# Spreading the first expert-table blocks over the second loop, pinning its last blocks, and laying the gate matrix out by tile of eight experts

## The chip, the cores and the metric

The kernel runs on one core of one Trainium2 chip. The metric is the device time of one execution in microseconds; the time before is the median of 3 runs.

## What is computed

A decoder block over 512 tokens of 1024 channels, all float32: a Conformer convolution and a sliding-window attention run beside each other, are merged by gates and added to the residual; then comes PEER, a mixer that picks experts by product keys. Cut to what matters here:

```python
h  = rmsnorm(x, norm1_g);  z = h @ w_in + b_in          # split into value, gate, q, k, v, two merge gates
x  = x + merged(conv, attention) @ w_out
h2 = rmsnorm(x, norm2_g)
q  = (h2 @ w_peer_q)                                     # 8 heads x 2 halves x 128
sc = einsum(q, sub_keys);  top 16 of each half; best 16 of their 256 sums -> expert_idx, gate (softmax)
a  = gelu(einsum("ced,cd->ce", u_emb[expert_idx], h2))   # 128 chosen of 16384 experts per token
x  = x + einsum("ce,ced->cd", gate * a, v_emb[expert_idx])
out = rmsnorm(x, final_g)
```

## The kernel before, in words

Tokens come in four blocks of 128. Every product is made in float32r from split operands: x = hi + lo, and a product is hi*hi + lo*hi + hi*lo. `load_w` fetches a 512 KB block of weights on SP's queue (`wraw`, 3 buffers), makes `whi` on ACT (L131) and `wlo` either on DVE (L137) or by an accumulating DMA from GpSimd (L134, L135, while `by_dma` is set); both have 4 buffers.

The first stage normalises the four token blocks, transposes them into `hT` and multiplies by `w_in` (42 blocks). The first two weight blocks go through `halves` (L159), which runs both over the first 256 tokens and then both over the second 256, so that TensorE begins before all of `hT` is there.

PEER treats the token blocks in two ways. Block 0 (`ROW_CHUNKS`) gathers its expert rows by indirect DMA (`by_rows`, L644): 128 slots over the `pu` table, each a multiply and sum on DVE (L651), a gelu, then 128 slots over the `pv` table, added up on DVE (L659) in `acc`, which starts as the residual `x2d`. Blocks 1 to 3 are dense: they multiply by all 16384 experts in 128 blocks of 128.

- U block i (`u_pieces`, L671): 24 matmuls of 384 columns over `put[i]`, gelu into `ga[i]`. 43 buffers of `ga` let U run ahead of V.
- The gate matrix: for each dense block, `build_g` (L599) builds 128 x 128 pictures of the softmax gates, four tokens a step, and stores 16 tokens at a time (`gst`, 2 buffers) to DRAM as `gb` (L632), 8 stores per block, 24 in all. `load_gates` (L679) brings back the part of eight experts (`gl`, 2 buffers), three loads per tile, one per dense block.
- V block i (`v_operands`, L687; `v_products`, L698): w = gate part times `ga[i]` on DVE (L690), split on ACT and DVE (L694, L695), then 18 matmuls of 512 columns over `pv[i]` (L701 to L703) that add into six PSUM banks `vacc` over all 128 blocks.

Order of work: eight heads (`head(h)`: scores on PE, L525; top 16 on DVE, L509 and on), each followed by `U_HEADS[h]` U blocks, 25 in all; then `keys` (L584) and `build_g` for three blocks, with 17 more U blocks threaded between the steps matmul by matmul and pinned in program order, so that 42 (`AHEAD`) are done; then 128 rounds. A round does one U block as long as there are any (rounds 0 to 85), one V block, and some slots of `by_rows`: 2.51 a round while there are U blocks, 1.03 after. The last two V blocks are taken together (L765) after the rows are finished and the residual of the three dense blocks has been loaded (L764). Then `vacc` is added (L774) and `finish` (L663) normalises and stores. The tile framework orders the instructions of each engine by a simulation of its own; program order and the dependencies are its input, and only pinned instructions keep their written order. Each engine and each DMA queue runs its instructions in order.

Of the kernel before, what the change touches and what calls it, by code (L numbers as in the profile page):

```python
# [9 lines left out]
F32 = mybir.dt.float32  # L10
# [3 lines left out]
AF = mybir.ActivationFunctionType  # L14
OP = mybir.AluOpType
AX = mybir.AxisListType

P = 128
D = 1024
KB = D // P  # L20
S = 512
# [12 lines left out]
ROW_CHUNKS = (0,)  # L34
# [4 lines left out]
CAND = 80  # L39

AHEAD = 42
U_HEADS = (4, 3, 3, 3, 3, 3, 3, 3)
U_PIECE = 3.6
ROWS = 4
GT = 16
GI = 8
R_G = 0.0
ROWS_U, ROWS_V = 1.48, 1.03
UC = 3
N_TAPS = 7  # L50
XT = 8
# [11 lines left out]
J_VAL, J_GATE, J_Q, J_K, J_V, J_GC, J_GA = 0, 8, 16, 24, 25, 26, 34  # L63
# [16 lines left out]
def body(ctx: ExitStack, tc: tile.TileContext, a, out):  # L80
    nc = tc.nc
# [4 lines left out]
    dram = ctx.enter_context(tc.tile_pool(name="dram", bufs=1, space=bass.MemoryType.DRAM))  # L86
# [7 lines left out]
    x2d = [dram.tile([P, D], F32, name=f"x2d{b}") for b in range(NB)]  # L94
    h2d = {b: dram.tile([P, D], F32, name=f"h2d{b}") for b in ROW_CHUNKS}
    NG = P // GT
    gv = {}
    for b in BUILT:
        gv[b] = dram.tile([P, NG, P, GT], F32, name=f"gb{b}")

    ident = const.tile([P, P], F32, name="ident")
    pc = const.tile([P, C_N], F32, name="pc")
# [9 lines left out]
    pace = [None]  # L112
# [43 lines left out]
        products(p, w, x)  # L156
        return p

    def halves(srcs, x):  # L159
        w = [load_w(t) for t in srcs]  # L160
        ps2 = [psum("mm") for _ in srcs]
        for c in (slice(0, S // 2), slice(S // 2, S)):
            for p, v in zip(ps2, w):
                products(p[:, c], v, [t[:, :, c] for t in x])
        return ps2
# [30 lines left out]
    def chunk(b):  # L196
        return slice(b * P, (b + 1) * P)
# [10 lines left out]
    warm = small.tile([P, 1], F32, name="warm", bufs=1)  # L208
# [16 lines left out]
    hT = pair_x("hT")  # L225
# [76 lines left out]
    def glu(j):  # L302
        if j >= UC:
            conv(KB * TAPS, j - UC)
        if j == 0:
            ps0 = halves([a["w_in"][J_GATE], a["w_in"][J_VAL]], hT)
            by_dma[0] = True
        pg = ps0[0] if j == 0 else zblock(J_GATE + j)
        sg = fr.tile([P, S], F32, name="sg")
        nc.scalar.activation(sg, pg, AF.Sigmoid, bias=bias(J_GATE + j))  # L310
        pv = ps0[1] if j == 0 else zblock(J_VAL + j)
        uc = fr.tile([P, HALO + S], F32, name="uc", bufs=UC)
        nc.vector.memset(uc[:, :HALO], 0.0)
        nc.vector.scalar_tensor_tensor(uc[:, HALO:], pv, bias(J_VAL + j), sg, op0=OP.add, op1=OP.mult)
        ucs[j] = uc
# [110 lines left out]
    p = psum("ot")  # L426
# [4 lines left out]
    for j in range(KB):  # L431
# [4 lines left out]
        else:  # L436
            nc.scalar.activation(sq, y[:, j], AF.Square)
            nc.vector.tensor_tensor(ysum, ysum, sq, op=OP.add)
    p = psum("ot")
    nc.tensor.matmul(p, ones, ysum, start=True, stop=True)  # L440
    r = rstd_of(p, D, [fr.tile([P, S], F32, name="ln_v", tag="qs", bufs=2),
                       fr.tile([P, S], F32, name="ln_t", tag="sg"),
                       fr.tile([P, S], F32, name="ln_r", tag="qs", bufs=2)])
# [7 lines left out]
    for j in range(KB):  # L451
        p = mm_block(a["w_ao"][j], oT)
        nc.vector.tensor_tensor(sga[:, j], sga[:, j], p, op=OP.mult)
    mT = pair_y("m")
    for j in range(KB):
        p = mm_block(a["w_co"][j], yT)
# [142 lines left out]
    def build_g(b):  # L599
        n = BUILT.index(b)  # L600
        p = psum("tr")
        nc.tensor.transpose(p[:, :P], gate[:, b], ident)
        gT = rt.tile([P, P], F32, name="gT", bufs=2)
        nc.scalar.activation(gT, p[:, :P], AF.Copy)
        high = P // LOW
        for g in range(P // GT):
            if g * GT % XS == 0:
                xa = gp.tile([P, XS, high], F32, name="xa")
                xb = gp.tile([P, XS, LOW], F32, name="xb")
                cs = slice(g * GT, g * GT + XS)  # L610
                for t, w, k in ((xa, high, 0), (xb, LOW, 1)):
                    nc.vector.tensor_tensor(t, keyT[:, k, n, cs, None].to_broadcast([P, XS, w]),
                                            iota[:, None, :w].to_broadcast([P, XS, w]), op=OP.is_equal)
                nc.vector.tensor_tensor(xa, xa, gT[:, cs, None].to_broadcast([P, XS, high]), op=OP.mult)
            st = gp.tile([P, P, GT], F32, name="gst", bufs=2)
            for t0 in range(0, GT, XT):
                c = slice(g * GT + t0, g * GT + t0 + XT)
                cx = slice(c.start % XS, c.start % XS + XT)
                yt = gp.tile([P, XT, P], F32, name="yt", tag="yt", bufs=XB)
                nc.vector.tensor_tensor(yt, keyT[:, 2, n, c, None].to_broadcast([P, XT, P]),  # L620
                                        iota[:, None, :].to_broadcast([P, XT, P]), op=OP.is_equal)
                xt = gp.tile([P, XT, high, LOW], F32, name="xt", tag="xt", bufs=XB)
                nc.vector.tensor_tensor(xt, xa[:, cx, :, None].to_broadcast([P, XT, high, LOW]),
                                        xb[:, cx, None, :].to_broadcast([P, XT, high, LOW]), op=OP.mult)
                for t1 in range(0, XT, 4):
                    p = psum(("sc", "ot")[t1 // 4 % 2]).rearrange("p (t i) -> p t i", t=4)
                    for t in range(4):
                        nc.tensor.matmul(p[:, t], yt[:, t1 + t], xt[:, t1 + t].rearrange("p a b -> p (a b)"),
                                         start=True, stop=True)
                    nc.scalar.activation(st[:, :, t0 + t1:t0 + t1 + 4].rearrange("p i t -> p t i"), p, AF.Copy)  # L630
                    yield
            nc.sync.dma_start(gv[b][:, g], st)  # L632

    def gathered(table, b, s):
        r = rows.tile([P, D], F32, name="row", bufs=ROWS)
# [8 lines left out]
    def by_rows():  # L644
        for b in ROW_CHUNKS:
            h = rows.tile([P, D], F32, name="hrow", tag="acc")
            nc.sync.dma_start(h, h2d[b])
            dots = small.tile([P, SLOTS], F32, name="dots", bufs=1)
            for s in range(SLOTS):
                r = gathered(a["pu"], b, s)  # L650
                nc.vector.scalar_tensor_tensor(r, r, 1.0, h, op0=OP.mult, op1=OP.mult, accum_out=dots[:, s:s + 1])  # L651
                yield
            nc.scalar.activation(dots, dots, AF.Gelu)
            nc.vector.tensor_tensor(gate[:, b], dots, gate[:, b], op=OP.mult)
            acc = rows.tile([P, D], F32, name="acc", tag="acc")
            nc.sync.dma_start(acc, x2d[b])
            for s in range(SLOTS):
                r = gathered(a["pv"], b, s)
                nc.vector.scalar_tensor_tensor(acc, r, gate[:, b, s:s + 1], acc, op0=OP.mult, op1=OP.add)  # L659
                yield  # L660
            finish(b, acc)

    def finish(b, acc):  # L663
        o = wp.tile([P, D], F32, name="wraw", bufs=WRAW)
        rmsnorm(o, acc, gf)
        nc.sync.dma_start(out[chunk(b), :], o)
# [12 lines left out]
    def load_gates(i, blocks=range(ND)):  # L679
        if i < P:  # L680
            if 0 in blocks:
                gl[i // GI] = vp.tile([P, NU // GT, GI, GT], F32, name="gl", bufs=2)
            for n in blocks:
                b = DENSE[n]
                nc.sync.dma_start(gl[i // GI][:, n * NG:(n + 1) * NG], gv[b][:, :, i:i + GI, :])

    def v_operands(i):  # L687
        v = load_w(a["pv"][chunk(i), :])
# [6 lines left out]
        nc.vector.tensor_tensor(wl3, w, wh3.bitcast(F32), op=OP.subtract)  # L695
        return v, (wh, wl)

    def v_products(i, n, v, w):  # L698
        for q in range(2):
            p, ns = vacc[2 * n + q], slice(q * 512, (q + 1) * 512)  # L700
            nc.tensor.matmul(p, w[0][:, chunk(n)], v[0][:, ns], start=(i == 0), stop=False)  # L701
            nc.tensor.matmul(p, w[0][:, chunk(n)], v[1][:, ns], start=False, stop=False)  # L702
            pace[0] = nc.tensor.matmul(p, w[1][:, chunk(n)], v[0][:, ns], start=False, stop=(i == P - 1))  # L703

    def v_steps(*steps):
        ops = [(i, v_operands(i)) for i in steps]
        for n in range(ND):
            for i, (v, w) in ops:
                v_products(i, n, v, w)

    ups = iter(range(P))

    def up(n):
        for _ in range(n):
            i = next(ups, None)
            if i is not None:
                for _ in u_pieces(i, load_w(a["put"][i])):
                    pass
# [31 lines left out]
    due = 0.0  # L750
    load_gates(0)
    last = {}
    for i in range(P):
        up(1)
        if 0 <= i % GI - GL_AT < ND:
            load_gates(i - i % GI + GI, (i % GI - GL_AT,))
        if i < P - 2:
            v_steps(i)
        elif i == P - 2:
            for _ in rowgen:  # L760
                pass
            for n, b in enumerate(DENSE):
                last[n] = rows.tile([P, D], F32, name="row", bufs=ROWS)
                nc.sync.dma_start(last[n], x2d[b])  # L764
            v_steps(i, i + 1)  # L765
        due += ((ROWS_U if i + AHEAD < P else 0.0) + ROWS_V) * len(ROW_CHUNKS)
        while due >= 1:
            due -= 1
            next(rowgen, None)
# [59 lines left out]
```

## Time and profile before

| | |
|---|---|
| median of 3 runs | 1771.82 us (1771.04 to 1774.27) |
| the profiled execution | 1772.01 us, span 1770.2 us |
| PE (TensorE matmul) busy | 1707.9 us, 96% of the span |
| DVE (VectorE) busy | 1355.1 us, 77% |
| ACT (ScalarE) busy | 898.5 us, 51% |
| GpSimd busy | 461.3 us, 26% |
| DMA | 444.86 MB, mean 251 GB/s |

The span runs from the first to the last instruction of the profiled execution; its time has another 1.8 us around it. The share of busy time is a mean over stages with different limits. PEld is PE's weight load, which overlaps PE. The clock in a row is the share of full speed that was granted to TensorE, whose two levels are 1.2 and 2.4 GHz.

### The profile page before, as it was taken

To read this page: it belongs to the slowest core of one execution; us is meant where nothing else is said; L and a number is where in the kernel's file an instruction comes from. 1 tells how busy PE (TensorE), PEld (TensorE's weight loads), DVE (VectorE), ACT (ScalarE), POOL (GpSimd) and SP (SyncE) were. 2 spreads that over 40 slices of the span, in tenths; PEclk is the share of its full clock that TensorE was granted. 3 is DMA by queue.
4 is the path that set the end of the run, shared out by engine and by line. 5 is a ranking of instruction groups with operands and counts; after the bars stand their busy time and mean duration, and the time that the engine had idled before them with its cause. 6 is when DMAs were issued, how large, how long until landed. Compare 5 with 4: busy or idle time off the path is not lost. (4 is left out here: it accounts for less than half of the span.)

```text
span 1770.2 us, 24879 instructions
## 1 busy us (share of the span) xinstructions
PE 1707.9 (96%) x8892; PEld 1504.4 (85%) x8892; DVE 1355.1 (77%) x2659; ACT 898.5 (51%) x1287; POOL 461.3 (26%) x374
## 2 busy tenths in 40 slices
PE   7999999999999996999899999999999999999996
PEld 6887777788899996999799999999999999977875
DVE  6999994545589998887677777777868778777775
ACT  6448999654656565887333333333333333333332
POOL 1111010110111110000334434433434534344330
PEclk9999998999999998999999999999999999999998
DMA  8996553885999994988889989888879889788873
GB/s 240 231 223 148 134 125 71 191 229 174 248 229 211 215 211 121 282 277 286 293 283 335 320 290 315 320 289 320 316 271 333 302 307 331 284 300 296 299 275 128
DMA packets 165708, 444.86 MB, mean 251 GB/s; under 512 B 14544, under 2 KB 66256, under 8 KB 162512
## 3 DMA queue, kind: packets, MB, share of 16 engines
q0 software_dynamic: 53280, 194.01, 41.2%
q1 hardware_dynamic: 112304, 249.26, 39.3%
q8 instruction: 70, 1.15, 0.3%
q14 instruction: 54, 0.44, 0.1%
HBM read 410.44 MB, written 29.88 MB: 249 GB/s over the span
## 5 line engine op out<-in xcount | busy, mean ns | idle before, releaser
L131 ACT ACTIVATE whi<-wraw 128x1024 fp32r<-128x1024 f32 x346 | 365.3, 1057 | 378.0 <-PE mm L146 188.7
L146 PE MATMUL mm<-tTh,whi 128*128 128x384 f32 (+2 forms) x1168 | 398.4, 342 | 1.5 <-ACT wlo L134 1.4
L146 PE MATMUL mm<-tTl,whi 128*128 128x384 f32 (+2 forms) x1168 | 398.6, 342 | 0.2 <-DVE tTl L194 0.2
L137 DVE TENSOR_TENSOR wlo<-wraw,whi 128x1024 fp32r<-128x1024 f32 x232 | 282.7, 1222 | 68.4 <-ACT whi L131 54.5
L636 POOL DMA_INDIRECT row<-pv,eidx x128 | 185.6, 1450 | 268.4 <-DVE acc L659 257.7
L636 POOL DMA_INDIRECT row<-pu,eidx x128 | 176.5, 1379 | 271.3 <-DVE row L651 243.3
L146 PE MATMUL mm<-tTh,wlo 128*128 128x384 f32 (+2 forms) x1168 | 240.5, 341 | 0.1
L694 ACT ACTIVATE wh<-gl 128x384 fp32r<-128x384 f32 x128 | 67.1, 525 | 329.8 <-PE ot L702 289.0
L146 PEld LDWEIGHTS mm<-tTh,whi 128*128 128x128 f32 x1168 | 220.0, 188 | 10.0 <-ACT wlo L134 1.8
L146 PEld LDWEIGHTS mm<-tTl,whi 128*128 128x128 f32 x1168 | 219.8, 188 | 8.3 <-DVE tTl L194 0.4
L146 PEld LDWEIGHTS mm<-tTh,wlo 128*128 128x128 f32 x1168 | 202.9, 188 | 4.2 <-DMA wlo<-w_pq 0.3
L659 DVE SCALAR_TENSOR_TENSOR acc<-row,gate,acc 128x1024 f32<-128x1024 f32 x128 | 164.0, 1282 | 12.3 <-DMA row<-pv,eidx 7.7
L296 DVE SCALAR_TENSOR_TENSOR yconv<-uc,pc,yconv 128x512 f32<-128x512 f32 x240 | 169.0, 746 | 0.4
L651 DVE SCALAR_TENSOR_TENSOR row<-row,hrow 128x1024 f32<-128x1024 f32 x128 | 154.4, 1220 | 8.6 <-DMA row<-pu,eidx 8.0
L146 PE MATMUL mm<-hTh,whi 128*128 128x512 f32 (+1 forms) x352 | 136.7, 391 | 1.1 <-ACT hTh L193 0.8
L146 PE MATMUL mm<-hTl,whi 128*128 128x512 f32 (+1 forms) x352 | 136.1, 389 | 1.4 <-DVE hTl L194 1.4
L690 DVE TENSOR_TENSOR gl<-gl,ga 128x384 f32<-128x384 f32 x128 | 62.0, 553 | 88.6 <-DMA gl<-gb 88.6
L134 ACT ACTIVATE wlo<-whi 128x1024 fp32r<-128x1024 f32 x114 | 120.2, 1055 | 9.7 <-PE mm L146 9.0
L695 DVE TENSOR_TENSOR wl<-gl,wh 128x384 fp32r<-128x384 f32 x128 | 71.0, 555 | 67.9 <-ACT wh L694 63.2
L701 PE MATMUL tr<-whi,wh 128*128 128x512 f32 x256 | 101.2, 397 | 9.1 <-ACT wh L694 5.3
L135 POOL DMA_DIRECT2D wlo<-w_in x40 | 34.9, 872 | 268.6 <-ACT wlo L134 212.3
L703 PE MATMUL tr<-whi,wl 128*128 128x512 f32 x256 | 96.4, 402 | 8.3 <-DVE wl L695 8.3
(255 smaller groups left out, 3174.1 us busy)
## 6 DMA issues: line engine op xcount, KB each, us to landing
wraw<-put SPq DMA_DIRECT2D x128, 512.0 KB
wraw<-pv SPq DMA_DIRECT2D x128, 512.0 KB
gb<-gst SPq DMA_DIRECT2D x24, 1024.0 KB
gl<-gb SPq DMA_DIRECT2D x48, 512.0 KB
wraw<-w_in SPq DMA_DIRECT2D x42, 512.0 KB
wlo<-put POOLq DMA_DIRECT2D x42, 512.0 KB
wlo<-w_in POOLq DMA_DIRECT2D x40, 512.0 KB
wraw<-w_out SPq DMA_DIRECT2D x16, 512.0 KB
```

The source lines that it names most:

```text
L131: nc.scalar.activation(hi, raw, AF.Copy)
L134: nc.scalar.activation(lo, hi.bitcast(F32), AF.Copy, scale=-1.0)
L137: nc.vector.tensor_tensor(lo, raw, hi.bitcast(F32), op=OP.subtract)
L146: pace[0] = nc.tensor.matmul(p, v[:, k * P:(k + 1) * P], t, start=(n == 0), stop=(n == len(terms) - 1))
L296: nc.vector.scalar_tensor_tensor(y[:, j], uc[:, t:t + S], w, y[:, j], op0=OP.mult, op1=OP.add)
L636: ins = nc.gpsimd.indirect_dma_start(out=r, out_offset=None, in_=table, in_offset=bass.IndirectOffsetOnAxis(ap=eidx[:, ROW_CHUNKS.index(b) ...
L651: nc.vector.scalar_tensor_tensor(r, r, 1.0, h, op0=OP.mult, op1=OP.mult, accum_out=dots[:, s:s + 1])
L659: nc.vector.scalar_tensor_tensor(acc, r, gate[:, b, s:s + 1], acc, op0=OP.mult, op1=OP.add)
L694: nc.scalar.activation(wh3, w, AF.Copy)
L695: nc.vector.tensor_tensor(wl3, w, wh3.bitcast(F32), op=OP.subtract)
L701: nc.tensor.matmul(p, w[0][:, chunk(n)], v[0][:, ns], start=(i == 0), stop=False)
L703: pace[0] = nc.tensor.matmul(p, w[1][:, chunk(n)], v[0][:, ns], start=False, stop=(i == P - 1))
```

## The change

The U blocks that are not yet done when V begins (86) are spread over 126 rounds at 86.5/126 a round, in place of one a round in the first 86. Row slots go at one rate, 2.07 a round. The heads get 3, 3, 3, 3, 3, 2, 3, 5 U blocks. `halves` can take other cuts, and the first use takes three: 128, 128 and 256 tokens. `gb` lies in DRAM by tile of eight experts, so that a load of `gl` reads 4 KB in one piece for each of 128 partitions, and a store writes 16 pieces of 512 bytes for each. In `by_rows` the first V slot writes `acc` with a multiply, and the residual is loaded and added at the end. In `v_products` the last two V blocks are ordered by bank (n, then q, then block), and pinned. After the last U block, ACT runs a Square and a Sqrt on one column.

```diff
-U_HEADS = (4, 3, 3, 3, 3, 3, 3, 3)
+U_HEADS = (3, 3, 3, 3, 3, 2, 3, 5)
-ROWS_U, ROWS_V = 1.48, 1.03
+ROWS_V = 2.07
...
-        gv[b] = dram.tile([P, NG, P, GT], F32, name=f"gb{b}")
+        gv[b] = dram.tile([P, P // GI, NG, GI, GT], F32, name=f"gb{b}")
...
-    def halves(srcs, x):
+    def halves(srcs, x, cuts=(slice(0, S // 2), slice(S // 2, S))):
...
-        for c in (slice(0, S // 2), slice(S // 2, S)):
+        for c in cuts:
...
-            ps0 = halves([a["w_in"][J_GATE], a["w_in"][J_VAL]], hT)
+            ps0 = halves([a["w_in"][J_GATE], a["w_in"][J_VAL]], hT,
+                         (chunk(0), chunk(1), slice(S // 2, S)))
...
-            nc.sync.dma_start(gv[b][:, g], st)
+            nc.sync.dma_start(gv[b][:, :, g], st.rearrange("p (a i) t -> p a i t", i=GI))
...
-            nc.sync.dma_start(acc, x2d[b])
             for s in range(SLOTS):
                 r = gathered(a["pv"], b, s)
-                nc.vector.scalar_tensor_tensor(acc, r, gate[:, b, s:s + 1], acc, op0=OP.mult, op1=OP.add)
+                if s == 0:
+                    nc.vector.tensor_scalar(acc, r, gate[:, b, s:s + 1], None, op0=OP.mult)
+                else:
+                    nc.vector.scalar_tensor_tensor(acc, r, gate[:, b, s:s + 1], acc, op0=OP.mult, op1=OP.add)
                 yield
+            r = rows.tile([P, D], F32, name="row", bufs=ROWS)
+            nc.sync.dma_start(r, x2d[b])
+            yield
+            nc.vector.tensor_tensor(acc, acc, r, op=OP.add)
             finish(b, acc)
...
-                nc.sync.dma_start(gl[i // GI][:, n * NG:(n + 1) * NG], gv[b][:, :, i:i + GI, :])
+                nc.sync.dma_start(gl[i // GI][:, n * NG:(n + 1) * NG], gv[b][:, i // GI])
...
+    def v_products(i, n, q, v, w, pin):
+        p, ns = vacc[2 * n + q], slice(q * 512, (q + 1) * 512)
+        for t, (wk, vk) in enumerate(((0, 0), (0, 1), (1, 0))):
+            pace[0] = nc.tensor.matmul(p, w[wk][:, chunk(n)], v[vk][:, ns], start=(i == 0 and t == 0),
+                                       stop=(i == P - 1 and t == 2))
+            if pin:
+                tc.keep_in_program_order(pace[0])
+
+    def v_steps(*steps, pin=False):
         ops = [(i, v_operands(i)) for i in steps]
         for n in range(ND):
-            for i, (v, w) in ops:
-                v_products(i, n, v, w)
+            for q in range(2):
+                for i, (v, w) in ops:
+                    v_products(i, n, q, v, w, pin)
...
+    ahead, share, tabled = AHEAD, 0.0, []
     for i in range(P):
-        up(1)
+        share += (P - AHEAD + 0.5) / (P - 2)
+        while share >= 1 or ahead <= min(i + 1, P - 1):
+            share -= 1
+            ahead += 1
+            up(1)
...
-        elif i == P - 2:
+        if ahead >= P and not tabled:
+            tabled.append(i)
+            nc.scalar.activation(warm, ga[P - 1][:, 0:1], AF.Square)
+            nc.scalar.activation(warm, warm, AF.Sqrt)
+        if i == P - 2:
...
-            v_steps(i, i + 1)
-        due += ((ROWS_U if i + AHEAD < P else 0.0) + ROWS_V) * len(ROW_CHUNKS)
+            v_steps(i, i + 1, pin=True)
+        due += ROWS_V * len(ROW_CHUNKS)
```

## Rows read from the trace of the kernel before

**Rows 1.** Waits of PE, whole span: us in total, times, longest.

```profile
PE tr L596 <- DVE k_p L592: 13.2, 2, 10.2
PE tr L703 <- DVE wl L695: 8.3, 4, 3.0
...
PE tr L701 <- ACT wh L694: 5.3, 1, 5.3
PE tr L701 <- ACT whi L131: 3.9, 1, 3.9
```

**Rows 2.** Windows: length, busy us of PE, PEld, DVE, ACT, POOL; clock, DMA, GB/s.

```profile
857.00:862.00 5.00, 5.00 (x12) 3.98 (x13) 5.00 (x10) 1.63 (x3) 0.00 (x0) 0.50 0.89 291
1564.00:1744.00 180.00, 171.69 (x738) 140.21 (x736) 133.03 (x154) 59.10 (x80) 58.90 (x41) 0.98 0.79 276
1747.00:1753.00 6.00, 5.13 (x12) 4.03 (x13) 4.26 (x8) 1.76 (x2) 0.00 (x0) 0.51 0.22 90
```

**Rows 3.** Waits of DVE from 1564 to 1744 us.

```profile
DVE gl L690 <- DMA gl<-gb: 25.1, 4, 7.5
```

**Rows 4.** Timeline of DVE at the first V block: start, us, instruction, [idle before].

```profile
855.72 3.84 DVE L690 TENSOR_TENSOR gl<-gl,ga 128x384 f32<-128x384 f32 x8 [8.62 <-DMA gl<-gb]
```

**Rows 5.** DMA queues, 1572.5 to 1575 us: packets, MB, share of 16 engines.

```profile
q1 hardware_dynamic: 1482, 0.75, 100.0%
```

**Rows 6.** DMA queues, 836.5 to 838.5 us, while a store of `gb` runs.

```profile
q1 hardware_dynamic: 109, 0.88, 103.8%
```

**Rows 7.** DMA queues, 848 to 851 us, gathers beside loads of `gl`.

```profile
q0 software_dynamic: 313, 1.15, 93.7%
q1 hardware_dynamic: 218, 0.11, 12.0%
```

**Rows 8.** Timeline of SP's queue behind the first loads of `gl`.

```profile
843.35 7.64 SPq L647 DMA_DIRECT2D hrow<-h2d  x1
```

**Rows 9.** Waits of DVE in the heads, 466 to 690 us.

```profile
DVE sv L509 <- PE sc L525: 21.9, 15, 6.2
```

**Rows 10.** Timeline of DVE before the scores of head 1 and of head 4.

```profile
504.64 0.30 DVE L509 MAX8 sv<-sc 128x8 f32<-128x128 f32 x1 [5.45 <-PE sc L525]
...
580.32 0.30 DVE L509 MAX8 sv<-sc 128x8 f32<-128x128 f32 x1 [1.40 <-PE sc L525]
```

**Rows 11.** Timeline of PE at the start, and the first plain f32 products.

```profile
12.65 1.97 PE L192 MATMUL tr<-ident,h 128*128 128x128 f32 x8 [2.49 <-DVE hTl L194]
...
22.67 1.03 PE L192 MATMUL tr<-ident,h 128*128 128x128 f32 x8
...
27.95 0.39 PE L146 MATMUL mm<-hTl,whi 128*128 128x256 f32 x1 [0.22 <-DVE hTl L194]
...
686.92 2.08 PE L628 MATMUL sc<-xt,yt 128*128 128x128 f32 x8 [0.44 <-DVE xt L623]
```

**Rows 12.** Window of the building of the gate matrix (columns as in rows 2).

```profile
690.00:840.00 150.00, 150.00 (x1133) 150.00 (x1133) 125.25 (x127) 123.12 (x141) 11.26 (x13) 1.00 0.83 264
```

**Rows 13.** The tile `gst`: its stores, and idle time of its engines until.

```profile
L632 SPq DMA_DIRECT2D gb<-gst x24: 319/320/327, 695.7 to 835.5; - x24
...
  DMA gb<-gst: 18.0, 14
```

**Rows 14.** Timeline of SP's queue at the end.

```profile
1731.44 6.86 SPq L764 DMA_DIRECT2D row<-x2d  x3
```

**Rows 15.** Timeline of ACT at the end.

```profile
1745.37 1.28 ACT L172 ACT_TABLE_LOAD   x1
...
1760.35 1.04 ACT L182 ACTIVATE wraw<-row 128x1024 f32<-128x1024 f32 x1
```

**Rows 16.** The chain that ended last: start, us, what.

```profile
1758.01 0.24 PE ot L703
```

**Rows 17.** Timeline of DVE at the end.

```profile
1758.86 1.28 DVE L774 TENSOR_TENSOR row<-row,ot 128x512 f32<-128x512 f32 x2
...
1765.10 1.29 DVE L184 SCALAR_TENSOR_TENSOR wraw<-row,n_r,g 128x1024 f32<-128x1024 f32 x1
```

More of the change, by code (lines that the diff above doesn't have):

```diff
@@ L696, in v_operands @@
         return v, (wh, wl)
[L698 to L705, printed above, removed]
+    def v_products(i, n, q, v, w, pin):
[6 more added lines that the diff above has]
+    def v_steps(*steps, pin=False):
         ops = [(i, v_operands(i)) for i in steps]
         for n in range(ND):
-            for i, (v, w) in ops:
-                v_products(i, n, v, w)
+            for q in range(2):
+                for i, (v, w) in ops:
+                    v_products(i, n, q, v, w, pin)
     ups = iter(range(P))
```

## The prediction

> **What bounds the kernel now.** I read the list of waits of PE first, because PE is the engine that works in every stage: what it waits for can be won, the rest is its own work. The long waits that the change touches are four [rows 1]: 13.2 us in two pieces (10.2 the longer) before the transposes of `keys`, 5.3 us before the first V block, 8.3 us in four pieces inside the V blocks, 3.9 us before the last two V blocks. In the mixed stretch of U and V blocks the list names none.
>
> Second, the windows, because PE also loses speed after a wait. Behind the 5.3 us wait the granted clock is 0.50 for 5.0 busy us (the 1.2 GHz level), so some 2.5 us are lost; behind the 3.9 us wait it is 0.51 for 5.1 busy us, 2.5 again. In 1564 to 1744, where only V blocks are left (738 matmuls, 41 blocks of 18), the mean is 0.98 of 180 us: 3.6 us. There 180 - 8.3 - 3.6 leaves 168.1 us, 4.1 a block [rows 2].
>
> Third, what ended those waits. In 1564 to 1744 DVE stands still four times, 25.1 us in all, in front of L690 for the load of `gl` [rows 3]; PE's four waits are for `wl`, the operand DVE makes later. So DVE's lead covers (25.1 - 8.3) / 4 = 4.2 us of each stall and the rest reaches PE. L690 comes in bursts of eight, a whole `gl` tile, at the first V block too, where DVE stood still 8.6 us [rows 4]. The cause is the load: 512-byte pieces. One such packet costs 2.5 us x 16 engines / 1482 = 27.0 ns [rows 5], one of 8 KB 2.0 x 1.038 x 16 / 109 = 305 ns [rows 6]. Worse is company: while the row gathers run they take 93.7% of the engines and the small packets 12.0% [rows 7]. SP suffers too: behind the first `gl` loads a plain load took 7.64 us to issue [rows 8].
>
> **The change, part by part.**
>
> *U spread and `gl` in 4 KB pieces.* The share is 86.5/126 = 0.687 U blocks for each V block, so the last U block goes with V block 125 and the V-only stretch shrinks to the last two blocks. Its four waits should end, by two covers: the three loads of a tile are 384 packets rather than 3072, and two V blocks in three have a U block beside them (4.1 us more of PE work). Taking 8 KB packets' rate, 384 x 153 / 16 = 3.7 us of all engines against 3072 x 27 / 16 = 5.2, and no crowding out. Credit: 8.3 + 3.6 = 11.9. What's late next: the same burst of L690 now falls where every third V block has no U block; I take +1.0 (nothing below; above, the rival D).
>
> *First V block.* With those loads done soon after the last stores, the first `wh` is ready before PE finishes its left-over U matmuls. Credit 5.3 + 2.5 = 7.8; bounds 3 and 7.8.
>
> *U_HEADS.* The sum stays 25, so PE reaches the end of the heads at the same moment; what moves is DVE. DVE waits 21.9 us for scores in 15 pieces [rows 9]. Before head 1 it waits 5.45, before a usual head 1.40 [rows 10]; the difference, 4.05, is head 0's fourth U block. That block goes: 4.05 earlier. The other 13 waits make (21.9 - 6.2 - 5.45) / 6 = 1.7 a head. With one block fewer in head 5, heads 6 and 7 get scores sooner, but DVE can use only its idle time, 2 x 1.7. Credit 4.05 + 3.4 = 7.5; PE's 10.2 us wait becomes 2.7. Bounds 3 (if DVE's order holds it back) and 8.1 (two whole blocks). Five U blocks in a row are filled from a ring of four weight buffers; I cost their loads at nothing.
>
> *End.* Now three loads of `x2d` hold SP's queue from 1731.44 on, and the last V weights go out behind them [rows 14]; then ACT does the row finish's Square, a table load of 1.28 us and Sqrt before `whi` [rows 15]. After: rows end at 258 / 2.07 = V block 125, U block 127 gives PE 4.1 us of cover, and the table is loaded early. PE's 3.9 us becomes perhaps 1.0, and the low clock behind it mostly goes. Pinned order n, q, step: only one half of the last output is open at PE's end. Before, PE ended at 1758.01 + 0.24 = 1758.25 [rows 16], the last pair of additions at 1758.86 + 1.28 = 1760.14 [rows 17], 1.9 later; after, one half remains, 0.64 by that pair: 1.2 won. The third block's scaling then started at 1765.10, queued behind two others; its Square ended at 1760.35 + 1.04 = 1761.4 [rows 15], and the one-column steps between I estimate at 1.8 us when nothing interrupts them: 1.9 won. So 2.9 + 2.0 + 3.1; credit 8.0; bounds 2 and 9.
>
> *Three cuts at the start.* The first two cuts are 96 matmuls of 128 columns in place of 48 of 256. No float32r matmul of 128 columns is in the trace. The nearest row is the transpose, one pass of 128 columns with its own weight load: eight take 1.97 us at 12.65, 0.22 each after the first, and 1.03 at 22.67, 0.11 each [rows 11]. So 128 columns cost as much as 256 do. Starting at 12.65 + 1.97 = 14.6: 36 slow ones until 22.67, then 60 and the 16 transposes of the later chunks at 0.11, 8.4 us: 31.0, against 27.95 now for the second half [rows 11]. I take +3. Below: if cost went with columns, 73 would be done by 22.67 and the rest by 26: -2. Above: a plain f32 product, eight records for four, took 2.08 us at the low clock, 0.52 each, 0.26 at the high one [rows 11]: 15 until 22.67, 81 x 0.26 + 1.8 = 22.9: 45.5, +17.
>
> *Stores of the gate matrix.* Each of 24 becomes 2048 packets of 512 bytes: 2048 x 27.0 / 16 = 3.46 us of all engines against 128 x 305 / 16 = 2.44, if a written packet costs what a read one does. Together 24.4 us. The engines are busy 0.83 of 150 us in that stage, 124.5 [rows 12]; after, 148.9 of 150. ACT already waits 18.0 us for stores [rows 13], and PE for none of it, because four score banks lie between. I take +3; below 0, above all 24.4.
>
> *At nothing.* The first-slot multiply has the size of the one it replaces; the closing addition of `x2d` is one more DVE step of some 1.28 us, under DVE's idle time (133 of 180 us busy in the V-only stretch [rows 2]); up to three table loads of 1.28 us fall on ACT, 59 of 180 us busy there. Without that cover each would cost its own length.
>
> Sum: -11.9 - 7.8 - 7.5 - 8.0 + 1.0 + 3 + 3 = -28.2. The profiled execution took 1772.0 (span 1770.2), so 1743.8, **1744**; the median of before is 1771.8, the same within 0.2.
>
> **Rivals.**
>
> *A, the narrow matmuls cost like plain f32.* For: they carry f32 weights, and no row shows the cheap form below 256 columns. Against: the transposes of the same width with f32 operands are cheap [rows 11]. +17 instead of +3: 1758.
>
> *B, all of the stores' added work is on the path.* For: no reserve is left. Against: PE waits for none of today's 18.0 us. +24.4 instead of +3: 1765.
>
> *C, slower.* One mechanism: written 512-byte packets dearer than read ones. The engines are full at 27 ns, so each further ns adds 24 x 2048 / 16 = 3.07 us; the 28 us of gain and the 3 already counted are gone at 27 + 10 = 37 ns. Half as dear again, 40 ns, adds 13 x 3.07 = 40: 1744 - 3 + 40 = 1781. For: the trace has no such write, and the pieces lie 4 KB and 64 KB apart. Against: the reads of before step 64 KB from partition to partition as well and ran at 0.75 MB in 2.5 us, 300 GB/s [rows 5]. The Trainium skill (DMA: Bandwidth & Descriptors, section Latency and other measured facts) says that copies whose rows lie a large power of two apart in HBM run slower, and gives 207 GB/s for 512 KiB; by it, as an estimate, a 1 MB store would take 5.1 us, 40 ns a packet, and the time be rival C's. The trace's reads at 64 KB don't agree with such a loss.
>
> *D, the stalls only move.* If the loads land no sooner, 14 bursts stall DVE 6.3 us each, 2.1 beyond its lead; half of them meeting no U block cost 15: 1758. For: the bursts stay. Against: 8.6 us at the first V block came of crowding that 4 KB packets escape.
>
> **How the numbers follow.** Forecast 0.56, with its own range 1734 to 1755 (the bounds of heads, first block and end, -2 at the start, +8 for stores); A 0.12, D 0.12, B 0.07, C 0.08; 0.05 for the written order not being the order run, near 1770. Leaving out C and the last, and what lies below the forecast's own range: 1733 to 1766. What this kernel's runs can tell from no change is about 0.2%, 3.5 us. Faster by more: 0.56 + 0.12 + 0.12 + 0.07 = 0.87; within, 0.03 of the last; slower, C and the rest of the last, 0.10.
>
> **What would show it.** Right: no PE wait for `wl` between 900 and the end; the wait for `k_p` near 3 us; no wait of 5 us at the first V block; PE's second half of the first block starting near 31; the 24 stores still some 6 us apart. Wrong: stores further apart and PE waiting in that stage (B, C); matmuls of 128 columns 0.25 us apart at full clock (A); PE waits for `wl` about every 55 us (D).

## The result, and the profile after

The changed kernel takes 1758.07 us (median of 4 runs, 1756.06 to 1762.04), the kernel before 1771.84 beside it: ratio 0.992, interval 0.9908 to 0.9933. That is 13.8 us less, half of the 28.2 that the sum promised, and 14 us above the forecast of 1744. The profiled execution took 1756.06 us (span 1754.3) against 1772.01 (span 1770.2).

Cut at the same points, the two profiled executions stand so (first score matmul of the heads, first matmul of the build, last U matmul ahead of V, PE's end, the span's end):

| stretch | before | after | difference | predicted |
|---|---|---|---|---|
| to the heads | 474.65 | 478.26 | +3.6 | +3 |
| heads | 212.3 | 204.0 | -8.3 | -7.5 |
| build and left-over U | 164.8 | 172.4 | +7.6 | +3 |
| V to PE's end | 906.6 | 889.7 | -16.9 | -23.6 |
| tail | 11.95 | 9.95 | -2.0 | -3.1 |
| sum | | | -16.0 | -28.2 |

The waits of PE over the whole span, first those that answer to [rows 1] (us in total, times, longest):

```profile
PE mm L146 <- ACT whi L131: 6.4, 1, 6.4
PE tr L597 <- DVE k_p L593: 6.0, 3, 3.4
PE sc L629 <- ACT gst L631: 5.2, 3, 2.0
...
PE tr L708 <- ACT wh L701: 0.9, 1, 0.9
```

The 8.3 us of waits for `wl` and the 5.3 us before the first V block are gone, and the wait for `keys` has fallen from 13.2 to 6.0. Two are new: 6.4 us for the weights of a U block, and 5.2 us for `gst` in the build. The windows (columns as in [rows 2]) show the start of V, the mixed stretch and the place of the new wait:

```profile
855.00:860.00 5.00, 5.00 (x25) 4.32 (x24) 2.24 (x4) 0.52 (x1) 0.00 (x0) 1.00 1.02 406
1564.00:1718.00 154.00, 154.00 (x762) 137.80 (x760) 114.02 (x118) 52.84 (x71) 55.34 (x42) 1.00 0.82 285
1718.00:1729.00 11.00, 4.64 (x17) 4.26 (x16) 6.16 (x11) 5.27 (x7) 0.00 (x0) 0.69 0.82 282
```

V begins at full clock (1.00 against 0.50), and up to 1718 PE is busy in all of 154 us. Then it is busy in 4.64 of 11. What it waits for is seen on SP's queue (start, us, instruction), which answers to [rows 14]:

```profile
1690.83 0.33 SPq L125 DMA_DIRECT2D wraw<-pv  x1
1704.88 0.33 SPq L665 DMA_DIRECT2D row<-x2d  x1
1708.15 9.94 SPq L782 DMA_DIRECT2D row<-x2d  x3
1718.18 0.38 SPq L125 DMA_DIRECT2D wraw<-put  x1
```

From 1690.83 to 1718.18 no weight load is issued. Between them stand four loads of `x2d`, the first for the row block's closing addition (L665), three for the dense blocks (L782), each into a `row` buffer that the last row slots on DVE have to free first. The last two such slots:

```profile
1715.15 2.60 DVE L662 SCALAR_TENSOR_TENSOR acc<-row,gate,acc 128x1024 f32<-128x1024 f32 x2
```

They end at 1717.75, the third load of L782 is issued by 1718.09, and the last U block's `put` goes out behind it. PE begins that block late and at the low clock:

```profile
1724.74 0.69 PE L146 MATMUL mm<-tTh,whi 128*128 128x384 f32 x1 [6.36 <-ACT whi L131]
...
1728.10 0.51 PE L146 MATMUL mm<-tTh,whi 128*128 128x384 f32 x1
...
1728.81 0.34 PE L146 MATMUL mm<-tTl,whi 128*128 128x384 f32 x1
```

0.32 us apart until 1728.4, 0.18 after: twelve matmuls at the 1.2 GHz level, some 1.9 us lost. With 6.36 and 0.86 the end loses 9.1 us.

DVE is late for `gl` all the same. Its waits for these loads from 860 to 1716 us are ten, the longest 6.6 us:

```profile
DVE gl L697 <- DMA gl<-gb: 37.5, 10, 6.6
```

PE waits behind none of them. At the first V block DVE now waits 1.27 us, where it waited 8.62 [rows 4].

In the build, the tile `gst` (its stores with min, median and max ns of issue; idle time of its engines until them), as in [rows 13]:

```profile
L633 SPq DMA_DIRECT2D gb<-gst x24: 513/519/1614, 691.4 to 838.4; - x24
...
  DMA gb<-gst: 29.0, 15
```

ACT waits 29.0 us for stores (before 18.0), and part of it now gets through four score banks to PE.

At the start (PE, as in [rows 11]):

```profile
14.65 0.41 PE L146 MATMUL mm<-hTh,whi 128*128 128x128 f32 x1
14.87 0.41 PE L146 MATMUL mm<-hTl,whi 128*128 128x128 f32 x1
...
25.79 0.28 PE L146 MATMUL mm<-hTl,whi 128*128 128x128 f32 x1
25.90 0.27 PE L146 MATMUL mm<-hTh,whi 128*128 128x128 f32 x1
```

Matmuls of 128 columns begin 0.21 us apart at the low clock and 0.11 at the high one, as a transpose of that width does.

### The profile page after: what moved, and what is told of

Read it like the earlier page. It is cut to its first block, busy times and chain, and to the rows that moved or that the text cites. A ratio compares the mean times of both kernels' runs of the same rounds, so it can differ in the third digit from the quotient of the medians.

```text
span 1754.3 us, 24965 instructions
## 1 busy us (share of the span) xinstructions
PE 1706.4 (97%) x8940; PEld 1506.6 (86%) x8940; DVE 1357.9 (77%) x2660; ACT 905.8 (52%) x1293; POOL 434.7 (25%) x374
## 4 chain that ended last, share of the span: by engine, by line
PE 83%; DVE 6%; ACT 5%; DMA 5%; issue 1%; SPq 0%; ACTq 0%; DVEq 0%
PE mm L146 46%; PE tr L708 10%; PE sc L708 10%; PE ot L708 10%; DMA gb<-gst 3%; PE sc L629 1%; PE ot L629 1%; ACT gst L631 1%; DVE yconv L296 1%; PE sc L358 1%; DMA gl<-gb 1%; ACT whi L131 1%; PE sc L526 1%; DMA wraw<-pv 1%; PE tr L381 1%
## 5 line engine op out<-in xcount | busy, mean ns | idle before, releaser
L637 POOL DMA_INDIRECT row<-pu,eidx x128 | 170.6, 1333 | 269.8 <-DVE row L652 248.2
L637 POOL DMA_INDIRECT row<-pv,eidx x128 | 165.1, 1290 | 266.3 <-DVE acc L662 237.1
L146 PE MATMUL mm<-hTh,whi 128*128 128x512 f32 (+2 forms) x368 | 141.1, 387 | 0.2 <-ACT sg L311 0.2
L146 PE MATMUL mm<-hTl,whi 128*128 128x512 f32 (+2 forms) x368 | 139.9, 384 | 0.0
L708 PE MATMUL tr<-whi,wl 128*128 128x512 f32 x256 | 100.9, 395 | 0.1
L135 POOL DMA_DIRECT2D wlo<-put x42 | 36.3, 864 | 260.6 <-ACT wlo L134 228.7
L708 PE MATMUL tr<-wlo,wh 128*128 128x512 f32 x256 | 100.6, 393 | 0.0
```

The lines of the kernel that those rows point to most:

```text
L135: nc.gpsimd.dma_start(lo, src, accum_op=OP.add)
L146: pace[0] = nc.tensor.matmul(p, v[:, k * P:(k + 1) * P], t, start=(n == 0), stop=(n == len(terms) - 1))
L637: ins = nc.gpsimd.indirect_dma_start(out=r, out_offset=None, in_=table, in_offset=bass.IndirectOffsetOnAxis(ap=eidx[:, ROW_CHUNKS.index(b) ...
L708: pace[0] = nc.tensor.matmul(p, w[wk][:, chunk(n)], v[vk][:, ns], start=(i == 0 and t == 0), stop=(i == P - 1 and t == 2))
```

## The experiments

Two theories stand for the missing 14 us. *The end*: the close of the row block (its `x2d` loads on SP's queue, its steps on ACT) makes the last U block late, about 9 us. *The start*: three cuts cost more than 3 us. Rivals: the stores' 4.6 us too many are the larger part, or the parts of the change pay for the same waits twice. All were timed beside the kernel before.

**The `x2d` loads on GpSimd's queue.**

```diff
-            nc.sync.dma_start(r, x2d[b])
+            nc.gpsimd.dma_start(r, x2d[b])
-                nc.sync.dma_start(last[n], x2d[b])
+                nc.gpsimd.dma_start(last[n], x2d[b])
```

> The changed kernel with its four loads of x2d (the row block's residual and the three of the dense blocks) issued from GpSimd's queue in place of SP's. Theory: on SP they stand ahead of the last U block's and the last three V blocks' weights and wait for row buffers, which makes PE's 6.4 us wait before the last U block, the 0.9 us after it and some 1.9 us at the low clock; all of it goes: about 9 us less than the changed kernel, 1749. Rival: the weights come late for another reason (buffers, the row finish on ACT), a wait of over 4 us stays and the time is 1755 or more.

Measured 1758.7 us (1753.66 to 1760.81), ratio 0.9917 (0.9902 to 0.9933): no gain. Its waits of PE, and two groups of its narrow matmuls at the start:

```profile
PE mm L146 <- ACT whi L131: 3.4, 1, 3.4
PE tr L708 <- ACT wh L701: 3.3, 1, 3.3
```

```profile
36.17 1.91 PE L146 MATMUL mm<-hTh,wlo 128*128 128x128 f32 x8
40.85 1.12 PE L146 MATMUL mm<-hTh,wlo 128*128 128x256 f32 x8
```

The 6.4 us wait is halved, but a second one of 3.3 stands behind it. And at 36 us this execution still ran at the low clock: eight narrow matmuls in 1.91. The kernel after had reached the high level at 25. Two things differ at once, so this run alone decides nothing about the end.

**The old layout of the gate matrix in the kernel after.**

```diff
-        gv[b] = dram.tile([P, P // GI, NG, GI, GT], F32, name=f"gb{b}")
+        gv[b] = dram.tile([P, NG, P, GT], F32, name=f"gb{b}")
-            nc.sync.dma_start(gv[b][:, :, g], st.rearrange("p (a i) t -> p a i t", i=GI))
+            nc.sync.dma_start(gv[b][:, g], st)
-                nc.sync.dma_start(gl[i // GI][:, n * NG:(n + 1) * NG], gv[b][:, i // GI])
+                nc.sync.dma_start(gl[i // GI][:, n * NG:(n + 1) * NG], gv[b][:, :, i:i + GI, :])
```

> The changed kernel with the gate matrix in DRAM as before (stores of 8 KB pieces, loads of 512-byte pieces). Theory: the building stage gets its 7.6 us back (its four-token steps again 1.49 us apart, no PE wait for the copies into gst), the wait of 5 us and its low clock return at the first V block (7.8), and the loads of gl stall DVE 6 us at a time; in the mixed stretch PE then waits in some of 14 places, 1 to 2 us each. Sum 1758 to 1770. Rival: the layout is worth nothing where U blocks cover the loads, so the kernel is faster without it: 1750 to 1754.

Measured 1757.97 us (1755.68 to 1762.31), ratio 0.9921 (0.9906 to 0.9936): the new layout buys nothing here that the time shows. No wait for `wl` came back in the mixed stretch, so the spreading alone covers the loads. The first V block's wait did come back (3.3 us); the stores cost less, PE waits 1.1 us for `gst` instead of 5.2.

**Two cuts in the kernel after.**

```diff
-            ps0 = halves([a["w_in"][J_GATE], a["w_in"][J_VAL]], hT,
-                         (chunk(0), chunk(1), slice(S // 2, S)))
+            ps0 = halves([a["w_in"][J_GATE], a["w_in"][J_VAL]], hT)
```

> The changed kernel with the first products cut at 256 and 256 tokens as before. Theory: the 128-column matmuls cost as much as 256-column ones, PE ran 3.9 us later from then on, and nothing downstream gave it back: 1754. Rival: the convolution's work on DVE sets the pace after it, and the 3.9 us are lost elsewhere: 1758.

Measured 1750.4 us (1748.67 to 1751.55), ratio 0.9875 (0.9859 to 0.9892): 7.7 us faster than the kernel after, where 4 were expected. At its end the wait for `whi` is 7.9 us.

**`U_HEADS` alone**, in the kernel before.

```diff
-U_HEADS = (4, 3, 3, 3, 3, 3, 3, 3)
+U_HEADS = (3, 3, 3, 3, 3, 2, 3, 5)
```

> The kernel before with the new U_HEADS alone. Theory: PE's wait for keys shrinks from 13 to some 6 us and the building stage begins 8 us earlier; everything after keeps its length: 1764. Rival: the building stage, which begins with less weight fetched ahead, gives part of it back: 1767 or more.

Measured 1763.26 us (1761.46 to 1767.37), ratio 0.9957 (0.9942 to 0.9971), as expected.

**The layout alone**, in the kernel before (the same lines as above, the other way round).

> The kernel before with the gate matrix in tiles of eight experts alone (its stores and its gl loads), against 1771.8 us. Stores: between +3 (predicted) and +7.6 (build stretch of the kernel after). First V block: its 5.3 us wait and the 2.5 us of low clock go, -7.8. The rival readings differ on the V-only stretch at the end (8.3 us of waits and 3.6 us at the low clock). If those waits came from gl loads crowded by the row gathers, the tiled loads remove them as well, and layout and spreading pay for the same thing twice: 1771.8 + 5.5 - 7.8 - 11.9 = 1758. If they came from the value weights, they stay: 1771.8 + 5.5 - 7.8 = 1769.5.

Measured 1760.24 us (1756.37 to 1761.82), ratio 0.9925 (0.9908 to 0.9942). Its waits of PE in V:

```profile
PE tr L703 <- DVE wl L695: 5.1, 3, 3.1
PE tr L701 <- ACT whi L131: 3.9, 1, 3.9
```

The first V block's wait is gone; of the 8.3 us for `wl` 5.1 are left, and the clock no longer falls there, only at the end. The time is near the first case, but not by its theory: in pieces of 4 KB the loads still stop DVE four times between 1564 and 1744 us, for 22.0 us in all, where it was 25.1 [rows 3].

```profile
DVE gl L690 <- DMA gl<-gb: 22.0, 4, 7.0
```

These 3.1 us less of DVE are the 3.2 us less of PE. So 512-byte pieces were not what made these loads late; what did is open.

**The spreading alone**, in the kernel before.

```diff
-ROWS_U, ROWS_V = 1.48, 1.03
+ROWS_V = 2.07
...
+    ahead, share = AHEAD, 0.0
     for i in range(P):
-        up(1)
+        share += (P - AHEAD + 0.5) / (P - 2)
+        while share >= 1 or ahead <= min(i + 1, P - 1):
+            share -= 1
+            ahead += 1
+            up(1)
...
-        due += ((ROWS_U if i + AHEAD < P else 0.0) + ROWS_V) * len(ROW_CHUNKS)
+        due += ROWS_V * len(ROW_CHUNKS)
```

> The kernel before with the U blocks spread (and the even row pace that goes with it) alone. The waits and the low clock of the V-only stretch go, -11.9, the first V block, the heads and the tail stay. If the last x2d loads hold up the weights of the last U block only because of the closing add's own late x2d load, which is not in here, the end stays at its 6.4 us: 1760. If any late U block stands behind them, the end grows by some 3 us: 1763. If spreading buys nothing by itself: 1771.8.

Measured 1759.35 us (1757.09 to 1759.61), ratio 0.9925 (0.991 to 0.994). In V only these waits of PE are left:

```profile
PE mm L146 <- ACT whi L131: 3.9, 1, 3.9
PE tr L701 <- ACT wh L694: 3.4, 1, 3.4
```

So spreading removes all of the waits for `wl` by itself. The 3.4 us are the first V block's, the 3.9 the last U block's. The time is that of the first case expected, but its condition is not met: the row block has its residual from the start here, and yet the last U block's `put` stands behind the three loads of the dense blocks:

```profile
1707.54 11.89 SPq L769 DMA_DIRECT2D row<-x2d  x3
1719.52 0.38 SPq L125 DMA_DIRECT2D wraw<-put  x1
```

So a late U block stands behind such loads with or without the closing addition. What ends its wait is ACT. From the last `wh` through the row block's Square, table load and Sqrt to `whi` it is 2.98 us, 1720.85 to 1723.83 here and 1743.80 to 1746.78 in the kernel before, and PE waits 3.9 us in both.

```profile
1723.83 1.04 ACT L131 ACTIVATE whi<-wraw 128x1024 fp32r<-128x1024 f32 x1
```

**Two cuts, and `x2d` on GpSimd's queue**, in the kernel after: both edits from above.

> The kernel after with two cuts in the first product and the x2d loads on GpSimd's queue. With two cuts the late rise of the clock is out of the way, so the x2d change is read against the two-cut kernel (1750.4 us). There the end lost 7.9 us to the wait and 2.9 us to the low clock; with the x2d loads on GpSimd's queue it lost 6.7 us in two waits and some 3.4 us to the clock, and V to the end of TensorE took 890.3 instead of 893.0 us. So 1750.4 - 2.7 = 1747.7. Rival, that SP's queue was all of it and the two waits were an accident of that run: 1750.4 - 10.8 = 1739.6. Rival, the x2d loads cost nothing: 1750.4.

Measured 1750.21 us (1746.89 to 1751.92), ratio 0.987 (0.9849 to 0.989): the same as two cuts alone, and the same two waits of PE at the end as in the first experiment, 3.4 us for `whi` and 3.1 for `wh`. The last U block's `put` is issued at 1695.69 now and its `pv` at 1698.64, and yet PE waits. ACT shows why:

```profile
1713.14 1.06 ACT L182 ACTIVATE wraw<-acc 128x1024 f32<-128x1024 f32 x1 [3.08 <-DVE acc L666]
...
1714.72 1.28 ACT L172 ACT_TABLE_LOAD   x1
1716.02 0.20 ACT L172 ACTIVATE n_t<-n_v 128x1 f32<-128x1 f32 x1
1716.13 1.99 ACT L131 ACTIVATE whi<-wraw 128x1024 fp32r<-128x1024 f32 x2
```

ACT stands still 3.08 us for DVE's closing addition of the row block, then does that block's Square, a table load and the Sqrt, and converts the weights only at 1716.13. So SP's queue is not the whole of it: with the weights loaded in time, the close of the row block still stands ahead of them on ACT. The close reaches into the second wait too: the last two `pv` loads go out only at 1719.67, since the row block's result takes one of the three `wraw` buffers and DVE frees the next, with `wlo`, behind that block's scaling. And the early table load that the change added stands ahead of the last `wh`:

```profile
1729.13 1.28 ACT L775 ACT_TABLE_LOAD   x1
...
1730.54 0.51 ACT L700 ACTIVATE wh<-gl 128x384 fp32r<-128x384 f32 x1
```

DVE had the operand of that `wh` ready at 1729.47 and PE begins at 1731.10, so the load, which the prediction had put at nothing, costs some 1 us here; no run takes it out alone. The 0.9 us for `wh` in the kernel after are of the same kind: operand ready at 1734.94, `wh` at 1736.01.

**Two cuts, and the row block done earlier**, in the kernel after, with two cuts as above.

```diff
-ROWS_V = 2.07
+ROWS_V = 2.20
```

The 258 steps then end at V block 258 / 2.20 = 117 instead of 125.

> The kernel after with two cuts and the row block's steps paced at 2.20 a V block instead of 2.07, so that its last gathers, its x2d load and its closing steps are done some seven V blocks before the last U block, and the last x2d loads find their buffers free. If the end's loss comes from the row block's close (x2d loads that hold SP's queue, and the close's steps ahead of the weight conversion on ScalarE), the 7.9 us wait and the 2.9 us of low clock go: 1750.4 - 10.8 = 1739.6. If the last U block's weights are late whatever the row block does: 1750.4. If the denser gathers starve the V blocks on the DMA engines (0.87 busy now): above 1755.

Measured 1741.74 us (1736.38 to 1742.65), ratio 0.9828 (0.9811 to 0.9845): 8.7 us faster than two cuts alone. SP's queue at the row block's close and at the last U block, its only wait of PE in V, and its last 65 us of V (columns as in [rows 2]):

```profile
1636.43 0.33 SPq L125 DMA_DIRECT2D wraw<-pv  x1
1643.95 0.33 SPq L664 DMA_DIRECT2D row<-x2d  x1
1645.61 10.70 SPq L781 DMA_DIRECT2D row<-x2d  x3
1656.40 0.39 SPq L125 DMA_DIRECT2D wraw<-pv  x1
...
1685.88 0.33 SPq L125 DMA_DIRECT2D wraw<-put  x1
```

```profile
PE tr L707 <- DVE wl L701: 0.2, 1, 0.2
```

```profile
1660.00:1725.00 65.00, 64.73 (x310) 55.88 (x308) 32.58 (x47) 28.53 (x40) 0.00 (x0) 1.00 0.36 122
```

Behind the close nothing but weights and the row block's store stands on the queue, the clock stays at 1.00, and with 0.2 us of waits in all of V the denser gathers starve nobody. The `x2d` loads hold the queue as long as before (10.70 us for the three, 9.94 in the kernel after), and here nothing waits. As an estimate from the rows of after: PE worked on for 27.5 us behind the last weight load (1690.83 to 1718.38) and began 6.6 us after the next one was issued (1718.18 to 1724.74), so a gap of some 21 us between weight loads costs nothing. In after it was 27.4 us, here it is 20.0.

**The same with the old layout.**

> The two-cut kernel with the row pace of 2.20 (1741.7 us) and the gate matrix in its old layout. Spreading the U blocks alone took 12 us off the kernel before, the layout alone 11, both together no more than that, so most of the layout's worth should be gone here: what is left to it is the first V block (3.3 us of wait and some 2 us at the low clock in the run of the kernel after with the old layout) against dearer stores (0 to 7.6 us in the build). From the heads to the end the layout was worth 2.8 us there: 1741.7 + 2.8 = 1744.5. If the layout pays nothing once the blocks are spread: 1741.7 or a little less. If the denser gathers make the old loads late again: above 1749.

Measured 1743.34 us (1742.25 to 1746.77), ratio 0.9844 (0.983 to 0.9858). The two intervals overlap; the layout's worth here, 1.6 us by the medians, is not told from nothing. PE waits 3.7 us at the first V block and 1.4 for `wl`; the build, from its first to its last matmul, is 146.6 us long against 147.6.

**The row block done earlier alone**, in the kernel after (three cuts kept, 2.20 for 2.07).

> The kernel after with the row pace of 2.20 instead of 2.07 and nothing else. It lost 6.36 + 0.86 us of waits and 1.9 us of low clock at the end, 9.1 in all; the same step took 8.7 us off the two-cut kernel. So 1758.1 - 8.9 = 1749.2. If the pace helped only because the start with two cuts left the end in another phase: no change, 1758.

Measured 1749.13 us (1745.64 to 1752.54), ratio 0.9878 (0.9862 to 0.9894): 8.9 us faster than the kernel after. The list of waits names none in V.

**Three cuts alone**, in the kernel before: the diff's lines of `halves` and of its first call, and nothing else.

> The kernel before with the first product in three cuts alone, against 1771.5 us. By the prediction's term, +3.0: 1774.5. By the two-cut run against the kernel after, +7.7: 1779, with a wide spread, since the first rise of the granted clock came 2.9, 8.7 and 17.8 us later in three profiles with three cuts. If the three cuts let the first half start early enough to pay for themselves: 1771.5 or less.

Measured 1779.28 us (median of 12 runs, 1770.12 to 1785.11), ratio 1.0041 (1.0024 to 1.0058): slower by 7.7 us. PE at its start:

```profile
22.57 1.93 PE L192 MATMUL tr<-ident,h 128*128 128x128 f32 x8
...
28.89 1.93 PE L192 MATMUL tr<-ident,h 128*128 128x128 f32 x8
30.89 1.06 PE L146 MATMUL mm<-hTh,wlo 128*128 128x128 f32 x8
```

Eight transposes take 1.93 us at 22.6 and still at 28.9, where they took 1.03 at 22.67 before [rows 11]. The high level comes at 30.8.

## Why the prediction was right and wrong

The direction was right and the time lies inside the range, but three terms carry the missing 14 us, and one of them had the wrong sign.

- **V-only stretch, -11.9: size right, cause half wrong.** No wait for `wl` is left, spreading alone does it, and the residual of +1.0 and rival D's stalls of PE about every 55 us did not appear. But the loads land little sooner, which was D's condition: the layout alone leaves DVE 22.0 of its 25.1 us, and in the kernel after DVE stops ten times, for up to 6.6 us. What works is the U block beside most V blocks, with which DVE can be late without PE noticing. The cause I named, 512-byte pieces, fits the first V block (DVE's wait from 8.62 to 1.27 us) and not this stretch. What I had not seen either is that the parts overlap: spreading alone gives 12.2 us (1771.5 - 1759.35), the layout alone 11.3, the heads 8.1, 31.6 added up. The two-cut kernel with the early row block has all three, and neither the 6.4 us lost at the end of the kernel before nor 2.0 of its tail, and is only 1771.5 - 1741.7 = 29.8 faster; with the old layout still 28.2. Of the layout's 11.3 some 6.8 are this stretch's (3.2 of waits, 3.6 of low clock), which spreading takes as well.
- **First V block, -7.8: right.** No wait, full clock, with the new layout only: with the old one 3.3 to 3.7 us of wait stay.
- **`U_HEADS`, -7.5: right.** -8.3 in the profile, 8.1 us as a change by itself (1771.4 - 1763.3). The waits left, 6.0 us, are 13.2 - 7.5 = 5.7 as worked out.
- **End, -8.0: the step that failed.** I read that `x2d` loads hold SP's queue, and then counted U block 127 as 4.1 us of cover. That block's own weights stand in the same queue behind the same loads: it was not cover but the first victim. Spreading had put it there. Instead of losing 1.5 us the end lost 9.1. Moving the loads to another queue was not the cure (0.2 us, within the spread); ending the row block eight V blocks earlier was (8.7 and 8.9 us in two kernels). So the cause is the close of the row block as a whole meeting the last U block: its late buffers hold SP's queue, and its steps stand ahead of the weights' conversion on ACT. Taking away the first leaves the second, which costs about as much; they are not two losses to be added. The early table load, put at nothing, comes on the path where PE has no other work left, for some 1 us.
- **Tail, -3.1 of the 8.0: -2.0.** The last scaling on DVE (1749.17) still comes 2.59 us behind the one before it (1746.58), with that block's one-column steps in between; I had let it start as soon as its own Square was done.
- **Three cuts, +3: price of the matmuls right, term mis-sized, 7.7.** The narrow matmuls cost what I took from the transposes, and the second half began at 31.89 in the profile of after (31 expected), so rival A is refuted, although its 1758 is the time measured: the number came out for other reasons. What I held fixed was the moment at which the clock rises. I took 22.67 from [rows 11]; with three cuts the high level came at 25 us in the kernel after, near 31 in three other runs, and at 40 in the first experiment, while all eight profiles with two cuts show it between 21 and 23.5. The heads follow: they begin at 478.3 us in the kernel after, between 481.5 and 483.4 in the three, at 485.4 in the first experiment, and between 473.5 and 475.8 with two cuts. From 25.2 to 40.1 the clock rises 14.9 us later and the heads begin 7.2 later, about half, as matmuls 0.21 us apart in place of 0.11 should give. The profiled execution of after was a mild one (+3.6), its median was not; that is why the profile seemed to confirm +3.
- **Stores, +3: right in kind, size loose.** Build and left-over U took 7.6 us more in the profile. From the first to the last build matmul it is 146.4 to 147.1 us in five runs with the old stores and 149.4 in a sixth; with the new ones it is between 147.6 and 154.8 in seven, 150.9 in the middle. Three pairs of runs differ in the layout alone: 3.5, 5.4 and 1.0 us, 3.3 in the mean, near what I took. I argued that PE waits for none of today's 18.0 us; with 29.0 us some reach it. Rivals B and C are refuted: a window in which only a store runs (packets, MB, share of 16 engines over 2 us) gives 2.0 x 1.148 x 16 / 1360 = 27.0 ns a written packet.

```profile
q1 hardware_dynamic: 1360, 0.70, 114.8%
```

The Trainium skill's rule on row pitch (DMA: Bandwidth & Descriptors, section Latency and other measured facts), by which rival C was priced, doesn't show at the 64 KB pitch of these writes: 348 GB/s. No run here has a pitch of 512 KiB. The same row gives 214 GB/s as the full rate of those copies, so its 207 at 512 KiB is hardly a loss, and the prediction read it as one.

In the profile 12.2 of the 28.2 us are missing. The end lost 9.1 where the sum had left 1.5, 7.6 more; the stores took 4.6 more, the tail 1.1, the start 0.6; the heads gave 0.8 more, and the residual of 1.0 did not come: 12.1. By medians 14.1 are missing (1758.1 - 1744), since the profiled execution is 2.0 faster than the median. Of these the end is 7.4 (1758.1 - 1749.1 less 1.5) and the three cuts 4.7 (7.7 less 3); with the tail, the heads and the residual that makes 11.6, and the rest, stores among it, is not settled. That the time lies in the range is luck in good part: 1758 is beyond the forecast's own 1734 to 1755, and the range reached 1766 for rivals A, B and D, none of which happened.

## What to carry to other kernels

Before a block of work is counted as cover for a wait, follow its own loads: if they stand in the queue that the wait comes from, it is not cover but late itself. When several parts of a change remove one wait, credit it once and look at what the last part adds on its own; here the layout is worth 1.6 us by the medians beside the spreading, not told from nothing, and leaving out one part (three cuts) and moving one number (2.07 to 2.20) took another 16 us off. A term that hangs on when the clock rises wants a range of executions, not one: the spread told of it (7.6 us over 17 runs of the kernel before, 15.0 over 12 with three cuts alone).

## What was not expected of the hardware

The granted clock rose late under narrow matmuls although PE was busy without a break: in the run with three cuts alone PE was busy in all of 12.4 to 31, in 128 columns at a time, and the low level lasted until 30.8 us. With two cuts in the kernel after PE was idle for 1.8 of the 10.6 us up to 23, and yet the high level came at 22.9. The two windows (columns as in [rows 2]):

```profile
12.40:31.00 18.60, 18.60 (x89) 18.49 (x90) 15.05 (x47) 10.67 (x16) 1.99 (x2) 1.00 0.84 236
```

```profile
12.40:23.00 10.60, 8.79 (x39) 7.99 (x40) 10.32 (x30) 7.19 (x9) 1.98 (x2) 1.00 0.75 233
```

Their clock column reads 1.00 all the same, evidently without the stretch at the start; the durations tell it here, 1.93 against 1.03 us for eight transposes. So of these two stretches the one in which PE was the fuller stayed low for longer; what delays the rise with three cuts, and why by another time in each execution, is open.

In the windows looked at, a queue with small packets got little beside one with large ones, for writes too. In 4 us behind a store's issue, with an accumulating load on GpSimd's queue, the kernel before and the kernel after moved (packets, MB, share of 16 engines):

```profile
q0 software_dynamic: 106, 0.43, 54.6%
q1 hardware_dynamic: 94, 0.77, 48.4%
```

```profile
q0 software_dynamic: 133, 0.52, 76.0%
q1 hardware_dynamic: 20, 0.01, 1.0%
```

With pieces of 8 KB the store had half of the engines from the start; with 512 bytes it had almost nothing until the other was through, although the engines were not full (76.0% and 1.0%). The Trainium skill (DMA: Bandwidth & Descriptors, section Queues, rings and completion order) says that each engine takes turns between its queues a packet at a time, and that such a packet is some 9 to 17 descriptors as a rule. The trace's packets are single pieces, so their counts do not test that rule. 106 to 94 would fit turns; nothing in turns alone gives 133 to 20.
